# Up projection: the products with the rounded weights and those with the remainders, alternating or in two groups

## The chip, the cores and the metric

The kernel runs on one core of a Trainium2 chip. The metric is the device time of one execution in microseconds (us), the median of several runs. The profile's engines are PE (TensorE: matrix products), PEld (its weight loads, which overlap the products), DVE (VectorE), ACT (ScalarE), POOL (GpSimd) and SP (SyncE, which here only starts transfers).

## What is computed

Two layers of an encoder over 256 positions with 2048 features, all in float32. Each layer has an attention part and then a gated feed-forward part. The change lies in the first product of the latter, `h2 @ w_up`:

```python
x = x + o @ w_out[l]
h2 = rms_norm(x, ln2_g[l])
u = depthwise_conv(h2 @ w_up[l], conv_w[l], conv_b[l])
gate, up = u[..., :D_FF], u[..., D_FF:]
x = x + (jax.nn.silu(gate) * up) @ w_down[l]
```

`w_up` has 2048 rows and 2 x 5632 columns in each layer.

## The kernel before

**Two parts for each number.** A float32 operand is split into a rounded part ("hi", in a format that PE multiplies fast) and the remainder ("lo", the same format). ACT writes the rounded part (line 112 for weights, 115 for activations) and DVE the remainder (113, 116). A product is the sum of hi x hi, lo x hi and hi x lo.

**The order of the weights.** All weights pass through one list of quanta of 1 MB, in the order in which they are used. SP loads a quantum into one of three `raw` buffers; each is split in two half blocks of 1024 columns (three for the kind "seven"), into `whi` and `wlo`, of which there are five buffers each. The loop at line 853 goes through the half blocks: it issues the split of the one four steps ahead, then the products of its own, then side work that is due (transposes, scores, sums of squares). The instructions are put in their final order on each engine by the framework's scheduler, which can move products of one half block past others. A buffer is free for the next split when the last product that reads it has run.

**The up projection** (`q_up`, line 527). A block `f` has 128 columns of the gate and 128 of the up part: two quanta, four half blocks. Its result is a PSUM tile `ps` of the tag `mm` (two buffers): for each of the two column groups `j` one bank of 512 columns, the first 256 for the products of two rounded parts, the second 256 for the two mixed products. In a half block, for each `j` and each of four slices `k` of 128 features, `two` (line 411) issues two products with the weights as the stationary operand and the activations `xs[k]` as the moving one:

- the rounded weights against both parts of `xs[k]`, 512 columns, into the whole bank;
- the remainders against the rounded part of `xs[k]`, 256 columns, added to the bank's second half.

Each product has its own weight load. There are 88 blocks in the two layers, so 352 half blocks, and in each eight products of 512 and eight of 256 columns.

**What follows a block** (`glu`, line 541): ACT copies the banks' first halves (545), DVE adds the second halves (546) and multiplies by the row factors r2 (547), POOL fills the edges, ACT and DVE do the convolution and the gate (555 to 561), and the result is split into `mid` buffers. ACT's first pass waits for the last product of the block.

**Around it.** The attention part runs its projections as products of 512 columns (`three`), and its scores (line 326, `thrice`) and values as products of 256 columns in the same fast format, in between. In the feed-forward part eight (at the end twelve) up blocks make a chunk; then comes the down projection of the chunk, with products of 512 columns only, where `mid` is stationary. The first up block of a layer starts while the last quarter of `x` is still being normalised: `turn_x` transposes it (149), `prep_x` splits it into `xs12` to `xs15`, and `stat_x` spreads r2 over the partitions by a product with ones (`pv<-tq,ones`).

Of the kernel before, what the change touches and what calls it, by code (L numbers as in the profile page):

```python
# [23 lines left out]
KD = D // P  # L24
# [35 lines left out]
def encoder_kernel(  # L60
# [36 lines left out]
    def mm(ps, lhsT, rhs, start, stop):  # L97
        nc.tensor.matmul(ps, lhsT, rhs, start=start, stop=stop, skip_group_check=True)  # L98
# [27 lines left out]
    xs = {}  # L126
# [281 lines left out]
    def at(q, f, *args, half=1):  # L408
        side.setdefault((q, half), []).append((f, args))

    def two(ps, w_h, w_l, mv, first, last):

        mm(ps, w_h, mv, first, False)
        mm(ps[:, 1], w_l, mv[:, 0], False, last)

    def three(ps, terms, hv, lv, first, last, apart=False):

# [109 lines left out]
    def q_up(l, f, u):  # L527
        def body(q, half, hi, lo):
            if u == 0 and half == 0:
                cur["up"] = psum.tile([P, 2, 2, T], F32, name="mm", bufs=2)  # L530
            ps = cur["up"]
            hv, lv = (w.rearrange("p (k j n) -> p k j n", k=4, j=2) for w in (hi, lo))
            for j in range(2):
                for kk in range(4):
                    k = 8 * u + 4 * half + kk
                    two(ps[:, j], hv[:, kk, j], lv[:, kk, j], xs[k], k == 0, k == KD - 1)
            if u == 1 and half == 1:
                glu(l, f, ps)
        return body

    def glu(l, f, ps):
        ux = halo[f % 2]
        r = T // GRID_W
        t = work.tile([P, 2, T], F32, name="prob", bufs=2)
        nc.scalar.activation(t, ps[:, :, 0], AF.Copy)  # L545
        nc.vector.tensor_add(t, t, ps[:, :, 1])  # L546
        nc.vector.tensor_mul(ux[:, :, r:r + T], t, st["r2"][:, None, :].to_broadcast([P, 2, T]))  # L547

        nc.gpsimd.tensor_copy(ux[:, :, 1:r], ux[:, :, T:T + r - 1])  # L549
        nc.gpsimd.tensor_copy(ux[:, :, T + r:T + 2 * r - 1], ux[:, :, r + 1:2 * r])  # L550
        y = work.tile([P, 2, T], F32, name="pT", bufs=4)
        for j in range(2):
            c = j * NF + f
            w0, w1, w2, b = (par["conv"][:, l, i, c:c + 1] for i in range(4))
            nc.scalar.activation(y[:, j, :], ux[:, j, r:r + T], AF.Identity, scale=w1, bias=b)  # L555
            for w, o in ((w0, 0), (w2, 2 * r)):
                nc.vector.scalar_tensor_tensor(y[:, j, :], ux[:, j, o:o + T], w, y[:, j, :],  # L557
                                               op0=ALU.mult, op1=ALU.add)
        nc.scalar.activation(t[:, 0, :], y[:, 0, :], AF.Silu)  # L559
        m = work.tile([P, T], F32, name="bias", bufs=2)  # L560
        nc.vector.tensor_mul(m, t[:, 0, :], y[:, 1, :])
        gs[f] = middle(l, f)
        split(gs[f][:, 0], gs[f][:, 1], m)
        ms[f] = m
        if f % 2 and f < NF - CHUNKS[-1] + PART:
            sums_mid(l, f // 2, ms.pop(f - 1), ms.pop(f))
# [265 lines left out]
    ps = psum.tile([P, T], F32, name="pv", bufs=1)  # L832
# [128 lines left out]
```

## Time and profile before

| | |
|---|---|
| median of 3 runs | 2092.12 us (2092.11 to 2092.13) |
| profiled execution | 2092.0 us, span 2090.2 us from the first to the last instruction |
| granted TensorE clock | 1.0 |
| up products with `whi` / `wlo` | 2816 / 2816 |
| up stretches, for example | 471.57 to 560.32 us, eight blocks |

Rows of groups give line, engine, operation, tiles written and read, shapes, count, busy time, mean ns of one and idle time of the engine before them. Rows of the timeline give start, duration, engine, line, operation and tiles, and how many equal instructions in a row are merged into one; the duration then reaches from the first start to the last end. Products are pipelined, so a product's duration is longer than the time until the next one starts. Rows of waits give who waited for whom, the total, how often and the longest.

### The profile page before, as it was taken

What the parts mean: (1) busy time and instruction counts of PE and PEld (TensorE: products, weight loads), DVE (VectorE), ACT (ScalarE), POOL (GpSimd) and SP (SyncE); (2) the same over time, 40 slices, a digit from 0 to 9 for tenths busy, and PEclk for the clock granted to TensorE, in tenths of its full rate; (3) what the DMA queues carried; (4) which work ended last, traced back from release to release, by engine and by line L of the source; (5) the groups of instructions that cost most, each with busy time, mean ns of one, the idle gap of its engine ahead of it and who ended that gap; (6) DMA issues with size and microseconds to landing.
All of it is one profiled execution on the core that took longest, in us unless ns stands there. A gap on an engine that the chain in (4) does not pass through costs nothing.

```text
span 2090.2 us, 29185 instructions
## 1 busy us (share of the span) xinstructions
PE 2083.5 (100%) x10816; PEld 1789.2 (86%) x10816; DVE 1720.5 (82%) x2604; ACT 1222.3 (58%) x1817; POOL 170.3 (8%) x237
## 2 busy tenths in 40 slices
PE   9999999999999999999999999999999999999999
PEld 8888888888888888888888888888888888888887
DVE  7786757898898988989757866678989989899896
ACT  7566556555555556556555665565556555555563
POOL 0011100100101001010000011001001010010100
PEclk9999999999999999999999999999999999999999
DMA  9544555556565564655655444555555655556554
GB/s 350 199 145 164 179 172 174 198 195 211 180 241 182 208 210 167 242 193 211 208 181 181 162 160 166 177 182 189 214 202 170 236 199 204 201 185 234 185 200 161
DMA packets 62144, 408.42 MB, mean 195 GB/s; under 512 B 7344, under 2 KB 9904, under 8 KB 13744
## 3 DMA queue, kind: packets, MB, share of 16 engines
q1 hardware_dynamic: 61280, 405.46, 56.2%
q8 instruction: 85, 1.39, 0.3%
q10 hardware_dynamic: 720, 1.08, 0.2%
q14 instruction: 59, 0.48, 0.1%
HBM read 404.42 MB, written 2.10 MB: 194 GB/s over the span
## 4 chain that ended last, share of the span: by engine, by line
PE 99%; DMA 0%; ACT 0%; DVE 0%; issue 0%
PE mm L98 90%; PE S L98 4%; PE pv L98 3%; PE tr L98 2%; PE tr L373 1%; PE tr L307 1%; PE S L149 1%; DMA head<-in_head 0%; ACT qtok L274 0%; ACT kT L315 0%; ACT xs L115 0%; DVE x L688 0%; ACT whi L112 0%
## 5 line engine op out<-in xcount | busy, mean ns | idle before, releaser
L112 ACT ACTIVATE whi<-raw 128x1024 fp32r<-128x1024 f32 (+1 forms) x797 | 830.9, 1057 | 689.9 <-PE mm L98 411.9
L113 DVE TENSOR_TENSOR wlo<-raw,whi 128x1024 fp32r<-128x1024 f32 (+1 forms) x797 | 963.9, 1220 | 270.3 <-ACT whi L112 231.8
L98 PE MATMUL mm<-xs,whi 128*128 128x512 f32 x2816 | 977.0, 390 | 0.0
L98 PE MATMUL mm<-xs,wlo 128*128 128x256 f32 x2816 | 794.1, 282 | 0.0
L98 PEld LDWEIGHTS mm<-xs,whi 128*128 128x128 f32 x2816 | 528.3, 188 | 110.5
L98 PEld LDWEIGHTS mm<-xs,wlo 128*128 128x128 f32 x2816 | 532.2, 189 | 1.1
L98 PE MATMUL mm<-whi,mid 128*128 128x512 f32 x1412 | 368.2, 391 | 0.0
L98 PEld LDWEIGHTS mm<-whi,mid 128*128 128x128 f32 x1412 | 263.0, 188 | 53.9
L98 PE MATMUL mm<-whi,xs 128*128 128x512 f32 x1152 | 294.2, 393 | 1.4 <-ACT qtok L274 1.3
L98 PEld LDWEIGHTS mm<-whi,xs 128*128 128x128 f32 x1152 | 213.1, 188 | 44.7 <-ACT qtok L274 1.8
L98 PE MATMUL mm<-wlo,mid 128*128 128x512 f32 x706 | 202.4, 392 | 0.0
L98 PE MATMUL mm<-wlo,xs 128*128 128x512 f32 x576 | 159.5, 393 | 0.0
L98 PEld LDWEIGHTS mm<-wlo,mid 128*128 128x128 f32 x706 | 132.1, 188 | 27.0
L557 DVE SCALAR_TENSOR_TENSOR pT<-halo,conv,pT 128x256 f32<-128x256 f32 x352 | 148.1, 478 | 0.9
L549 POOL COPY halo<-halo 128x6 f32<-128x6 f32 x88 | 39.6, 450 | 1232.6 <-DVE halo L547 1232.6
L98 PEld LDWEIGHTS mm<-wlo,xs 128*128 128x128 f32 x576 | 107.3, 188 | 21.6
L555 ACT ACTIVATE pT<-halo,conv 128x256 f32<-128x256 f32 x176 | 95.1, 587 | 5.8 <-DVE halo L547 5.7
L550 POOL COPY halo<-halo 128x6 f32<-128x6 f32 x88 | 77.1, 876 | 0.2 <-POOL halo L549 0.2
L547 DVE TENSOR_TENSOR halo<-prob,acc_b 128x512 f32<-128x512 f32 x88 | 60.6, 689 | 1.9
L546 DVE TENSOR_TENSOR prob<-prob,mm 128x512 f32<-128x512 f32 x88 | 59.8, 679 | 0.0
L545 ACT ACTIVATE prob<-mm 128x512 f32<-128x512 f32 x88 | 51.3, 583 | 7.1 <-PE mm L98 7.1
L559 ACT ACTIVATE prob<-pT 128x256 f32<-128x256 f32 x88 | 35.5, 404 | 30.0 <-DVE pT L557 30.0
(180 smaller groups left out, 1475.4 us busy)
## 6 DMA issues: line engine op xcount, KB each, us to landing
raw<-in_w_up SPq DMA_DIRECT2D x176, 1024.0 KB, 4.9
raw<-in_w_in SPq DMA_DIRECT2D x71, 1024.0 KB, 4.9
raw<-in_w_down SPq DMA_DIRECT2D x48, 1024.0 KB, 4.8
raw<-in_w_seven SPq DMA_DIRECT2D x40, 1024.0 KB, 4.9
raw<-in_w_out SPq DMA_DIRECT2D x32, 1024.0 KB, 4.9
raw<-in_w_plain SPq DMA_DIRECT2D x10, 1024.0 KB, 4.8
bias<-in_bias SPq DMA_DIRECT2D x16, 160.0 KB, 3.1
x<-in_x SPq DMA_DIRECT2D x4, 512.0 KB, 10.7
```

Source lines behind the costliest of these rows:

```text
L98: nc.tensor.matmul(ps, lhsT, rhs, start=start, stop=stop, skip_group_check=True)
L112: high = nc.scalar.activation(hi, src, AF.Copy)
L113: nc.vector.tensor_sub(lo, src, hi.bitcast(F32))
L149: nc.tensor.transpose(ps[:, j, tt * P:(tt + 1) * P], x[:, tt, (k + j) * P:(k + j + 1) * P], ident)
L545: nc.scalar.activation(t, ps[:, :, 0], AF.Copy)
L546: nc.vector.tensor_add(t, t, ps[:, :, 1])
L547: nc.vector.tensor_mul(ux[:, :, r:r + T], t, st["r2"][:, None, :].to_broadcast([P, 2, T]))
L549: nc.gpsimd.tensor_copy(ux[:, :, 1:r], ux[:, :, T:T + r - 1])
L550: nc.gpsimd.tensor_copy(ux[:, :, T + r:T + 2 * r - 1], ux[:, :, r + 1:2 * r])
L555: nc.scalar.activation(y[:, j, :], ux[:, j, r:r + T], AF.Identity, scale=w1, bias=b)
L557: nc.vector.scalar_tensor_tensor(y[:, j, :], ux[:, j, o:o + T], w, y[:, j, :], op0=ALU.mult, op1=ALU.add)
L559: nc.scalar.activation(t[:, 0, :], y[:, 0, :], AF.Silu)
```

## The change

In each half block of the up projection the eight products with the rounded weights are issued first, in the order of `j` and `k`, and then the eight with the remainders in the same order. Operands, banks, numbers of products and flags are the same.

```diff
-    def two(ps, w_h, w_l, mv, first, last):
-
-        mm(ps, w_h, mv, first, False)
-        mm(ps[:, 1], w_l, mv[:, 0], False, last)
+    def two(terms):
+
+        for ps, w_h, w_l, mv, first, last in terms:
+            mm(ps, w_h, mv, first, False)
+        for ps, w_h, w_l, mv, first, last in terms:
+            mm(ps[:, 1], w_l, mv[:, 0], False, last)
...
-            for j in range(2):
-                for kk in range(4):
-                    k = 8 * u + 4 * half + kk
-                    two(ps[:, j], hv[:, kk, j], lv[:, kk, j], xs[k], k == 0, k == KD - 1)
+            two([(ps[:, j], hv[:, kk, j], lv[:, kk, j], xs[k], k == 0, k == KD - 1)
+                 for j in range(2) for kk, k in enumerate(range(8 * u + 4 * half, 8 * u + 4 * half + 4))])
```

PE's order in the first half block of a layer's third up block, before:

```order
L98 MATMUL mm_3322<-xs0_2795,whi_3203 128x512
L98 MATMUL mm_3322<-xs0_2795,wlo_3204 128x256
L98 MATMUL mm_3322<-xs1_2798,whi_3203 128x512
L98 MATMUL mm_3322<-xs1_2798,wlo_3204 128x256
L98 MATMUL mm_3322<-xs2_2806,whi_3203 128x512
L98 MATMUL mm_3322<-xs2_2806,wlo_3204 128x256
L98 MATMUL mm_3322<-xs3_2809,whi_3203 128x512
L98 MATMUL mm_3322<-xs3_2809,wlo_3204 128x256
```

The same half block with the change; the rows shown are its second four products with `whi` and its first four with `wlo`:

```order
L98 MATMUL mm_3322<-xs0_2795,whi_3203 128x512
L98 MATMUL mm_3322<-xs1_2798,whi_3203 128x512
L98 MATMUL mm_3322<-xs2_2806,whi_3203 128x512
L98 MATMUL mm_3322<-xs3_2809,whi_3203 128x512
L98 MATMUL mm_3322<-xs0_2795,wlo_3204 128x256
L98 MATMUL mm_3322<-xs1_2798,wlo_3204 128x256
L98 MATMUL mm_3322<-xs2_2806,wlo_3204 128x256
L98 MATMUL mm_3322<-xs3_2809,wlo_3204 128x256
```

Runs of eight equal widths take the place of the alternation, in all half blocks but the first few of each layer, where other work is mixed in.

ACT's order at the start of the first layer's up stage, where the last slices of `x` are rounded (`xs12` to `xs15`) between the splits of coming weights, before:

```order
L112 ACTIVATE whi_3107<-raw_2947 128x1024
L115 ACTIVATE xs12_3090<-S_3085,head_72 128x256
L115 ACTIVATE xs14_3101<-S_3096,head_72 128x256
L112 ACTIVATE whi_3142<-raw_3010 128x1024
L115 ACTIVATE xs13_3093<-S_3085,head_72 128x256
L115 ACTIVATE xs15_3104<-S_3096,head_72 128x256
L112 ACTIVATE whi_3162<-raw_3010 128x1024
```

With the change:

```order
L112 ACTIVATE whi_3107<-raw_2947 128x1024
L112 ACTIVATE whi_3142<-raw_3010 128x1024
L115 ACTIVATE xs12_3090<-S_3085,head_72 128x256
L115 ACTIVATE xs14_3101<-S_3096,head_72 128x256
L115 ACTIVATE xs13_3093<-S_3085,head_72 128x256
L112 ACTIVATE whi_3162<-raw_3010 128x1024
L115 ACTIVATE xs15_3104<-S_3096,head_72 128x256
```

The split `whi_3142` moved ahead of the slices and `whi_3162` ahead of `xs15`.

ACT's order at the end of a chunk, where the last up block's first pass (`prob<-mm`) stands among splits of the down projection's weights and of sums (`mid<-tq`), before:

```order
L112 ACTIVATE mid_5154<-bias_5152 128x256
L112 ACTIVATE whi_5231<-raw_5078 128x1024
L545 ACTIVATE prob_5254<-mm_5172 128x512
L112 ACTIVATE mid_5162<-tq_5157 128x256
L112 ACTIVATE whi_5273<-raw_5078 128x1024
```

With the change:

```order
L112 ACTIVATE mid_5154<-bias_5152 128x256
L112 ACTIVATE whi_5231<-raw_5078 128x1024
L112 ACTIVATE mid_5162<-tq_5157 128x256
L545 ACTIVATE prob_5254<-mm_5172 128x512
L112 ACTIVATE whi_5273<-raw_5078 128x1024
```

The sum's split and the block's first pass changed places. The orders of SP and POOL are the same in both kernels.

## The prediction

> **What bounds the kernel now.** I read the page's first and fourth parts first, then the list of waits for PE and its weight loads, then single stretches of the timeline.
>
> ```profile
> PE 2083.5 (100%) x10816; PEld 1789.2 (86%) x10816; DVE 1720.5 (82%) x2604; ACT 1222.3 (58%) x1817; POOL 170.3 (8%) x237
> PE 99%; DMA 0%; ACT 0%; DVE 0%; issue 0%
> L98 PE MATMUL mm<-xs,whi 128*128 128x512 f32 x2816 | 977.0, 390 | 0.0
> L98 PE MATMUL mm<-xs,wlo 128*128 128x256 f32 x2816 | 794.1, 282 | 0.0
> L98 PEld LDWEIGHTS mm<-xs,wlo 128*128 128x128 f32 x2816 | 532.2, 189 | 1.1
> ...
> PE mm L98 <- ACT qtok L274: 1.3, 2, 0.7
> PE pv L98 <- DVE halfpi L94: 1.1, 1, 1.1
> ...
> PEld mm L98 <- ACT whi L112: 1.0, 3, 0.4
> ```
>
> PE is the whole chain, and it waits for other engines for 2.4 us in 2090, its weight loads for a little more. The two groups that the change reorders, 2816 products with the rounded weights (512 columns, called h here) and 2816 with the remainders (256 columns, called l), have no idle time before them. So nothing that ACT, DVE or a DMA delivers sooner can be worth anything here, and the question is only the pace at which PE starts products. The durations 390 and 282 ns are no pace: products overlap, so I count from start to start. The first two rows below are the first h of one up stretch and the first product after it, 256 pairs later; the next two stand 24 products of 512 columns apart in a down stretch.
>
> ```profile
> 471.57 0.39 PE L98 MATMUL mm<-xs,whi 128*128 128x512 f32 x1
> ...
> 560.32 1.08 PE L98 MATMUL mm<-whi,mid 128*128 128x512 f32 x4
> ...
> 1001.41 1.98 PE L98 MATMUL mm<-whi,mid 128*128 128x512 f32 x8
> ...
> 1006.85 1.52 PE L98 MATMUL mm<-whi,mid 128*128 128x512 f32 x6
> ```
>
> A pair takes (560.32 - 471.57) / 256 = 0.3467 us. A 512 among its like takes (1006.85 - 1001.41) / 24 = 0.2267, which leaves 0.1200 for an l in the alternation. The up stretches hold 2816 x 0.3467 = 976 us of the span. They are already the plain sum of their parts, with not one stall to win back.
>
> **The change part by part.** No product, load, split or DMA is added or removed. There are 2816 / 8 = 352 half blocks. In each, h l h l ... (8 x 0.3467 = 2.773 us) becomes eight h and then eight l. Fifteen changes of width become one inside, and one at the seam. The price is what eight l in a row take, and what eight h take right behind them. The up stretches hold almost no such runs, so I take the nearest ones: in the attention parts, scores and values run as 256s of the same format, each with its own weight load, and eight 512s follow.
>
> ```profile
> 112.14 0.28 PE L98 MATMUL S<-kTb,qT 128*128 128x256 f32 x1
> ...
> 112.86 2.00 PE L98 MATMUL mm<-whi,xs 128*128 128x512 f32 x8
> 114.70 1.07 PE L98 MATMUL mm<-wlo,xs 128*128 128x512 f32 x4
> ...
> 1153.34 0.28 PE L98 MATMUL S<-kTb,qT 128*128 128x256 f32 x1
> ...
> 1154.05 2.00 PE L98 MATMUL mm<-whi,xs 128*128 128x512 f32 x8
> 1155.89 1.07 PE L98 MATMUL mm<-wlo,xs 128*128 128x512 f32 x4
> ...
> 1226.73 1.98 PE L98 MATMUL mm<-whi,xs 128*128 128x512 f32 x8
> 1228.54 0.39 PE L98 MATMUL mm<-wlo,xs 128*128 128x512 f32 x1
> ```
>
> The last two rows are the control: eight 512s behind 512s take 1228.54 - 1226.73 = 1.81 us. Behind six 256s they take 114.70 - 112.86 = 1.84, and in the second layer 1155.89 - 1154.05 = 1.84. The six 256s themselves take 0.72 and 0.71, 0.120 each and a little less. Six l and eight h at the old paces are 0.720 + 1.813 = 2.533; these stretches take 2.56 and 2.55, so **+0.027 and +0.017 us**. The reader is to see that a run of narrow products costs nothing itself, and that the wide ones behind it are slow for a while. Two more such places give the ends.
>
> ```profile
> 101.92 0.28 PE L98 MATMUL S<-mid,qT 128*128 128x256 f32 x1
> ...
> 102.98 1.78 PE L98 MATMUL mm<-whi,xs 128*128 128x512 f32 x7
> 104.60 0.39 PE L98 MATMUL mm<-wlo,xs 128*128 128x512 f32 x1
> ...
> 127.90 0.87 PE L98 MATMUL pv<-pT,v_b 128*128 128x256 f32 x6
> 128.61 0.39 PE L98 MATMUL mm<-wlo,xs 128*128 128x512 f32 x1
> 128.84 2.01 PE L98 MATMUL mm<-whi,xs 128*128 128x512 f32 x8
> 130.70 1.07 PE L98 MATMUL mm<-wlo,xs 128*128 128x512 f32 x4
> ...
> 172.07 0.85 PE L98 MATMUL pv<-pT,v_b 128*128 128x256 f32 x6
> 172.76 1.99 PE L98 MATMUL mm<-whi,xs 128*128 128x512 f32 x8
> ```
>
> Nine 256s and seven 512s from 101.92: 2.68 against 9 x 0.120 + 7 x 0.2267 = 2.667, +0.013. Six and nine from 127.90: 2.80 against 2.760, **+0.040**, the upper end. The six from 172.07 take 0.69 (0.115 each), and seven starts among the eight behind them take 1.99 - 0.39 = 1.60 against 1.587: -0.030 + 0.013 = **-0.017**, the lower end. That last run stands right behind transposes, unlike the others.
>
> One disturbance of the kind stands in an up stretch itself, where the scheduler put two h in a row:
>
> ```profile
> 341.98 0.63 PE L98 MATMUL mm<-xs,whi 128*128 128x512 f32 x2
> ...
> 343.61 0.39 PE L98 MATMUL mm<-xs,whi 128*128 128x512 f32 x1
> ```
>
> Between these rows start five h and four l: 1.63 us against 5 x 0.2267 + 4 x 0.120 = 1.613, +0.017 for one broken alternation. So the same tiles react too. I take the mean of the two stretches that are nearest in form, six 256s and then exactly eight 512s: +0.022 us for a half block. The sum is 352 x 0.022 = 7.7 us, on the profiled execution's 2092.0 (span 2090.2 and 1.8 around it; the median, 2092.12, is the same): **2099.7 us**. The ends are 352 x 0.040 = +14.1 and 352 x -0.017 = -6.0.
>
> [...]
>
> What moves on other engines. The split of the weights is released earlier: the last read of a whi is now 8 x 0.120 = 0.96 us before the half block's end, and no reader needs it sooner. The first l comes seven h later than it did. Neither can add a wait in steady blocks, and PE shows none to remove. At the chunks' ends ACT rounds a sum (mid<-tq) ahead of the first pass of the last block's gate (prob<-mm), not behind it.
>
> ```profile
> 560.58 0.60 ACT L545 ACTIVATE prob<-mm 128x512 f32<-128x512 f32 x1 [0.70 <-PE mm L98]
> 561.08 0.41 ACT L112 ACTIVATE mid<-tq 128x256 fp32r<-128x256 f32 x1
> ...
> 561.89 0.68 DVE L546 TENSOR_TENSOR prob<-prob,mm 128x512 f32<-128x512 f32 x1
> ...
> 565.09 0.61 PE L98 MATMUL mm<-whi,mid 128*128 128x512 f32 x2
> ```
>
> ACT stood idle 0.70 us before prob, so mid's 0.41 fits there; and PE writes the freed bank only at 565.09, 2.5 us after DVE's read ends. I cost it at nothing. Without that cover it is at most 0.41 us at each of ten chunk ends, 4 us. At the start of each layer's up stage xs15 is now rounded behind one more whi and its subtraction.
>
> ```profile
> L112 ACT ACTIVATE whi<-raw 128x1024 fp32r<-128x1024 f32 (+1 forms) x797 | 830.9, 1057 | 689.9 <-PE mm L98 411.9
> L113 DVE TENSOR_TENSOR wlo<-raw,whi 128x1024 fp32r<-128x1024 f32 (+1 forms) x797 | 963.9, 1220 | 270.3 <-ACT whi L112 231.8
> ```
>
> That is 1.06 + 1.22 us later, but the order puts 19 h and 15 l of other work (19 x 0.2267 + 15 x 0.120 = 6.1 us) between PE's row for r2 and its first product with xs15: nothing, too, and at most 2 x 2.3 = 4.6 us if that cover failed.
>
> **The rivals.** *Order does not count* (0.33): with the runs regular and all from the same tiles, PE settles, and eight and eight take 2.773 us as before. For it: the alternation is the exact sum of its parts, and no wait is touched. Against it: every place above where 256s end has slow 512s behind it. It gives 2092.0, and holds as long as a half block gains or loses under 0.012 us (4.2 us in all, 0.2%, about what a measurement of this kernel tells from no change). That the scheduler undoes the change would give the same time, but PE's order shows the runs.
>
> *The l settle faster than 0.120* (0.08), the other side: eight in a row are long enough to reach the 0.115 of the run at 172.07, and the h behind lose only 0.013. It decides in the change's favour once eight l save more than the 512s lose, 0.03 us; at -0.017 a half block it gives 2086.0. Against it: the runs of six at 112.14 and of nine at 101.92 stay at 0.118 to 0.120.
>
> *Weight loads come into the open* (0.02): a load is 189 ns by its row, an l only 120. Were the loads of seven l in a row shown in full, it would be 352 x 7 x 0.069 = 170 us more, 2262. The runs of 256s, with a load each, exclude it nearly.
>
> **How the numbers follow.** The forecast, +0.013 to +0.040 a half block or 2096.6 to 2106.1, has 0.57. With the rivals that makes slower by over 0.2% 0.59, within it 0.33, faster 0.08. The range, 2086 to 2106, takes in both ends of the unknown price and the case of no change, and leaves out about 1 in 20. The likeliest case's own range is 2096.6 to 2106.1.
>
> **What would show it.** In the profile after, the eight h of a half block, from the first's start to the first l's, should take about 1.84 us, not 1.81, and the eight l 0.94 to 0.96; the waits of PE should stay near 2.4 us, and the stretches outside the up projection keep their lengths. If the h take 1.81 and the l 0.96, the second case holds; if the l take 0.92 or less, the third. A wait of PE for xs, mid or a bank would mean that a cover costed at nothing has failed. The forecast is wrong if the slow starts come from the change of tiles or formats around the attention's products and not from the change of width.

## The result, and the profile after

The changed kernel takes **2103.97 us**, the median of four runs (2103.80 to 2103.98); the kernel before took 2092.12 in the runs beside it (2092.11 to 2092.32). The ratio is 1.0056, with a 95% interval of 1.0040 to 1.0072: slower by 11.85 us. The forecast was 2099.7 in a range of 2086 to 2106.

The first fence has rows of the page of the changed kernel: engines, the chain that ended last, and the groups that the change reorders. The second has its list of waits for PE.

```profile
PE 2094.4 (100%) x10816; PEld 1781.5 (85%) x10816; DVE 1721.8 (82%) x2604; ACT 1224.6 (58%) x1817; POOL 109.8 (5%) x237
PE 99%; DMA 0%; ACT 0%; DVE 0%; issue 0%
L98 PE MATMUL mm<-xs,whi 128*128 128x512 f32 x2816 | 714.4, 395 | 0.0
L98 PEld LDWEIGHTS mm<-xs,whi 128*128 128x128 f32 x2816 | 504.2, 188 | 97.9
L98 PE MATMUL mm<-xs,wlo 128*128 128x256 f32 x2816 | 388.4, 280 | 0.0
```

```profile
PE mm L98 <- ACT qtok L274: 1.3, 2, 0.7
PE pv L98 <- DVE halfpi L94: 1.1, 1, 1.1
PE mm L98 <- ACT whi L112: 0.9, 1, 0.9
```

PE is still the whole chain, it waits for 3.3 us instead of 2.4, and the two groups have no idle time ahead of them. A weight load lasts 188 ns, as before, and lies beside the products. The busy times of the two groups fell by hundreds of us although the kernel is slower: overlapping products of one group are counted once, so busy time says nothing of the pace here. The timeline does. Its rows give start, duration, engine and operation, and how many equal ones are merged.

```profile
112.79 2.00 PE L98 MATMUL mm<-whi,xs 128*128 128x512 f32 x8
114.63 1.07 PE L98 MATMUL mm<-wlo,xs 128*128 128x512 f32 x4
...
472.44 2.03 PE L98 MATMUL mm<-xs,whi 128*128 128x512 f32 x8
...
480.85 2.03 PE L98 MATMUL mm<-xs,whi 128*128 128x512 f32 x8
482.72 1.10 PE L98 MATMUL mm<-xs,wlo 128*128 128x256 f32 x8
483.66 2.03 PE L98 MATMUL mm<-xs,whi 128*128 128x512 f32 x8
485.53 1.10 PE L98 MATMUL mm<-xs,wlo 128*128 128x256 f32 x8
486.46 2.03 PE L98 MATMUL mm<-xs,whi 128*128 128x512 f32 x8
...
562.25 1.09 PE L98 MATMUL mm<-whi,mid 128*128 128x512 f32 x4
```

From start to start, eight h take 1.87 us (482.72 - 480.85) and eight l 0.94 or 0.93 (483.66 - 482.72, 486.46 - 485.53): 0.2337 and 0.117 each. The forecast had reckoned with 0.2267 and 0.1200 for the kernel before. The mean of all starts in the traces, from here on "by all starts", gives 0.2284 and 0.1184 there, and 0.2333 and 0.1174 with the change. The up stretch of eight blocks is 562.25 - 472.44 = 89.81 us; it was 88.75. That is 0.033 for each of its 32 half blocks, 352 x 1.06 / 32 = 11.7 us in all, nearly the whole difference. The eight 512s of the attention part, on which the forecast leaned, take 1.84 us, as before.

So the h became slower by far more than the l became faster, and the h do not settle: all eight take about 0.2337. The question is why.

### The profile page after: what moved, and what is told of

Same layout as the page of the kernel before. It is cut to its first block, busy times and chain, and to the rows that moved or that the text cites. A ratio compares the mean times of both kernels' runs of the same rounds, so it can differ in the third digit from the quotient of the medians.

```text
span 2102.1 us, 29183 instructions
## 1 busy us (share of the span) xinstructions
PE 2094.4 (100%) x10816; PEld 1781.5 (85%) x10816; DVE 1721.8 (82%) x2604; ACT 1224.6 (58%) x1817; POOL 109.8 (5%) x237
## 4 chain that ended last, share of the span: by engine, by line
PE 99%; DMA 0%; ACT 0%; DVE 0%; issue 0%
PE mm L98 90%; PE S L98 4%; PE pv L98 3%; PE tr L98 2%; PE tr L373 1%; PE tr L307 1%; PE S L149 0%; DMA head<-in_head 0%; ACT qtok L274 0%; ACT kT L315 0%; ACT xs L115 0%; DVE x L688 0%; ACT whi L112 0%
## 5 line engine op out<-in xcount | busy, mean ns | idle before, releaser
L98 PE MATMUL mm<-xs,whi 128*128 128x512 f32 x2816 | 714.4, 395 | 0.0
L98 PEld LDWEIGHTS mm<-xs,whi 128*128 128x128 f32 x2816 | 504.2, 188 | 97.9
L98 PEld LDWEIGHTS mm<-xs,wlo 128*128 128x128 f32 x2816 | 380.3, 188 | 32.2
L98 PE MATMUL mm<-xs,wlo 128*128 128x256 f32 x2816 | 388.4, 280 | 0.0
L549 POOL COPY halo<-halo 128x6 f32<-128x6 f32 x88 | 31.5, 358 | 1305.0 <-DVE halo L547 1305.0
L747 DVE TENSOR_TENSOR raw<-raw 128x1024 f32<-128x1024 f32 x40 | 48.8, 1220 | 0.5
```

What stands on the lines that cost most here:

```text
L747: nc.vector.tensor_sub(w[:, 1:3], w[:, 1:3], w[:, 2:4])
```

## The experiments

All times are of the slowest and only core; the kernel before, on the same chips, took 2092.03 to 2092.27 in all of them.

### Shorter and longer runs

Four of each kind, and two of each kind (`terms` is the list that the changed kernel hands to `two`; three points stand for lines left out):

```diff
...
+            for i in range(0, 8, 4):
+                two(terms[i:i + 4])
```

> Groups of four in place of eight: for each j four products with whi, then four with wlo, twice the seams. Theory A (a wide product that runs within about nine starts after a narrow run goes at 0.2337 us, whatever the number of seams, and a narrow one in a run at 0.117): 4 x 0.2337 + 4 x 0.1175 twice = 2.81 us for a half block as in the changed kernel, 2102 to 2105 us. Theory B (each seam between the widths has a fixed price, 0.0335 us, the changed kernel's loss for a half block): twice the loss, 352 x 0.067 = 23.6 us, 2116 us.

```diff
...
+            for i in range(0, 8, 2):
+                two(terms[i:i + 2])
```

> Groups of two: h h l l all through. Theory A: the wide ones never settle; between 0.0067 us for each h h l l, as at 339.24 us of the kernel before, and the 0.0335 for a half block of the changed kernel: 2101 to 2104 us. Theory B (fixed price for a seam, now four in a half block): 352 x 0.134 = 47 us, 2139 us.

One run each: 2101.72 and 2108.45 us. By all starts, h take 0.2332 and l 0.1168 in groups of four, 0.2343 and 0.1178 in groups of two. A fixed price for each change of width is out: the loss would have doubled and quadrupled, to 23.6 and 47 us, and it is 9.6 and 16.3.

Sixteen of each (the remainders' products kept to the end of the quantum), and 32 of each (to the end of the block):

```diff
-    def two(terms):
+    late = []
+
+    def two(terms, end):
...
-        for ps, w_h, w_l, mv, first, last in terms:
-            mm(ps[:, 1], w_l, mv[:, 0], False, last)
+        late.extend(terms)
+        if end:
+            for ps, w_h, w_l, mv, first, last in late:
+                mm(ps[:, 1], w_l, mv[:, 0], False, last)
+            late.clear()
...
+            two(terms, half == 1)
```

> The products with wlo of two half blocks are issued together: sixteen h, then sixteen l. Theory A: the wide ones settle at 0.2267 after about nine, so they lose 9 x 0.005 to 0.007 = 0.045 to 0.06 us, and the narrow ones at 0.117 save 16 x 0.003 = 0.048: 0 to +0.015 a pair of half blocks, 2091 to 2095 us. Theory B: half the seams, half the loss: 2098 us. A third possibility, that consecutive wide products of these tiles are slow for good (0.2337): 16 x 0.007 - 0.045 = 0.067 a pair, 2104 us.

The version with 32 differs from it in one condition:

```diff
-            two(terms, half == 1)
+            two(terms, u == 1 and half == 1)
```

> The products with wlo of a whole block are issued together: 32 h, then 32 l. Theory A: the wide ones lose 0.045 to 0.06 us once, the narrow ones save 32 x 0.003 = 0.09 at 0.117, or, if they settle at 0.1133 after eight, up to 0.18: 88 blocks x -0.03 to -0.14 us = 2080 to 2089 us. Theory B: a quarter of the loss, 2095 us. Slow for good: 32 x 0.007 - 0.09 = +0.13, 2104 us. All of this if the longer life of wlo makes PE wait nowhere.

They take 2107.77 us (ratio 1.0075, 1.0058 to 1.0091) and 2132.14 (1.0190, 1.0175 to 1.0206). The timeline of the version with sixteen:

```profile
482.14 2.05 PE L98 MATMUL mm<-xs,wlo 128*128 128x256 f32 x16
484.02 3.89 PE L98 MATMUL mm<-xs,whi 128*128 128x512 f32 x16
487.75 1.45 PE L98 MATMUL mm<-xs,wlo 128*128 128x256 f32 x11
```

Sixteen h take 3.73 us, 0.2331 each, and sixteen l 1.88, 0.1175 each. A slow start that fades, which is what the forecast was made of, would show a lower mean in a longer run; it shows the same. The rest of these two versions' time lies outside the pace: by all starts, the products outside the up projection take 5.5 us more than in the changed kernel with sixteen and 27.5 us more with 32. With 32 the remainders are held longer, so their buffers come free later, and PE waits for splits, as its waits show:

```profile
PE pv L98 <- ACT whi L112: 9.8, 11, 1.0
PE S L98 <- DVE wlo L113: 6.8, 10, 0.7
```

The idea that the h are slow only behind narrow products falls here. What was left: wide products of these tiles, where they lie, are slow in a row, for good. Next I asked what about them it is.

### Neighbours, and one width alone

The alternation as before, but with each remainder product taken from another slice:

```diff
...
+            for i in range(0, 8, 4):
+                for kk in range(4):
+                    ps_j, w_h, _, mv, first, _ = terms[i + kk]
+                    mm(ps_j, w_h, mv, first, False)
+                    _, _, w_l, mv, _, _ = terms[i + (kk + 3) % 4]
+                    mm(ps_j[:, 1], w_l, mv[:, 0], False, kk == 3 and u == 1 and half == 1)
```

> In each half block and column group, products of 512 and 256 columns alternate as before the change, but each remainder product belongs to another slice k than the rounded ones beside it, so that no two neighbours read the same xs tile. Theory W (the pace of a product depends on the widths beside it): a pair takes 0.347 us as before the change, 2092. Rival O (a wide product is quick only because the product beside it reads the same xs tile; 0.2337 and 0.117 else, as in the runs of eight): 2104, and 2112 if the narrow ones stay at 0.120.

2092.06 us beside 2092.03. Its up stretch, by the first h and the first product behind it:

```profile
471.44 0.39 PE L98 MATMUL mm<-xs,whi 128*128 128x512 f32 x1
...
560.19 1.08 PE L98 MATMUL mm<-whi,mid 128*128 128x512 f32 x4
```

88.75 us, as before the change. That neighbours read the same `xs` is worth nothing.

All products wide, in the changed order:

```diff
-            mm(ps[:, 1], w_l, mv[:, 0], False, last)
+            mm(ps, w_l, mv, False, last)
```

> The changed order, but the remainders are multiplied with both parts of xs, 512 columns into the whole bank, so that all products of the up projection are 512 wide (this adds the product of two remainders to the first half). Theory W (it is the neighbourhood of narrow products that sets the pace): 16 uniform products in a half block at the 0.2267 us of the other stretches, 3.63 us, 2392 in all. Rival T (consecutive wide products of these tiles run at 0.2337 whatever is near): 3.74 us, 2432.

2441.26 us. PE now also waits for a row of sums, 9.7 us in all, as the waits and the timeline show:

```profile
PE mm L98 <- DVE tq L619: 9.7, 8, 1.5
```

```profile
381.20 2.03 PE L98 MATMUL mm<-xs,wlo 128*128 128x512 f32 x8
383.07 1.09 PE L98 MATMUL mm<-xs,whi 128*128 128x512 f32 x4
```

Without that wait it would be 2431.6, and eight wide products take 1.87 us with no narrow one near. So rival T's 2432 holds: the slow pace of the h needs no change of width.

All products narrow, in the order before:

```diff
+        mm(ps[:, 0], w_h, mv[:, 0], first, False)
+        mm(ps[:, 1], w_h, mv[:, 1], False, False)
         mm(ps[:, 1], w_l, mv[:, 0], False, last)
```

> The order before the change, but each product with the rounded weights is made as two of 256 columns, one for each part of xs, so that all products of the up projection are 256 wide, 24 in a half block. If narrow ones in a row run at the 0.117 us that they take in runs of eight: 2103. If at 0.120, as in the alternation: 2129. If the 512s' 0.2267 is two halves without a cost of their own: 0.1133, 2072.

2104.35 us, the first of the three cases. The two rows are 13 times three products apart:

```profile
479.79 0.28 PE L98 MATMUL mm<-xs,wlo 128*128 128x256 f32 x1
...
484.33 0.28 PE L98 MATMUL mm<-xs,wlo 128*128 128x256 f32 x1
```

4.54 / 39 = 0.1164 us. Here 256 columns take half of 0.2337, nearly: uniform products in the up stage of these kernels go at one rate per column, and that rate is not the one of the other stages.

### The place of the weights

In the up stage alone, the split weights do not begin at the start of their buffers but `UP_AT = 56` columns behind it (line 53, used at 756), 224 bytes. Buffers of `whi` and `wlo` stand 1088 columns apart, 4352 = 17 x 256 bytes, and the tiles `xs` and `mid` whole multiples of 2048. So the distance from the moving operand to the stationary one, within 256 bytes, is the same for every product of a stage: 0 for the wide products of the attention and down parts, 224 in the up part. The changed kernel at 0:

```diff
-UP_AT = 56
+UP_AT = 0
```

> The changed kernel with the split weights at the start of their buffers in the up stages too, not 56 columns behind it. If the place of the weights against the activations is what makes consecutive wide products slow (rival P): the wide ones go back to 0.2267 us while the narrow ones keep 0.117, 20 us less, 2084. If the place does not matter: 2104 as the changed kernel.

2099.02 us, beside 2092.03: neither case. The timeline:

```profile
480.68 2.00 PE L98 MATMUL mm<-xs,whi 128*128 128x512 f32 x8
482.52 1.11 PE L98 MATMUL mm<-xs,wlo 128*128 128x256 f32 x8
483.48 2.00 PE L98 MATMUL mm<-xs,whi 128*128 128x512 f32 x8
...
489.06 2.00 PE L98 MATMUL mm<-xs,whi 128*128 128x512 f32 x8
```

Eight h take 1.84 us and eight l 0.96; three half blocks take 489.06 - 480.68 = 8.38, 2.793 each, 0.020 over the 2.773 of before, and 352 x 0.020 = 7.0 us is the whole difference. This is the attention part's behaviour, which the forecast had taken for granted: by the trace's starts, in both, the h settle from 0.236 at most to 0.227 over five products, and the 256s take 0.120. It appears in the up stage once the weights have the attention part's place.

Then two kernels with many places, and with room made for moving the `xs` too:

```diff
-UP_AT = 56
+UP_AT = (40, 0, 2, 4, 6, 8, 10, 12, 14, 24, 32)
+XS_AT = 8
...
-        xs[k] = act.tile([P, 2, T], F32R, name=f"xs{k}")
+        o = XS_AT if which == 1 and l == 1 else 0
+        xs[k] = act.tile([P, 2 * T + 16], F32R, name=f"xs{k}")[:, o:o + 2 * T].rearrange("p (a t) -> p a t", a=2)
...
-            o = UP_AT if kind == "up" else 0
-            hl[s] = tuple(wp.tile([P, 1024 + 64], F32R, name=t, bufs=SPLIT_AHEAD + 1)[:, o:o + 1024]
+            o = UP_AT[ups.index(s) % 176 // 16] if kind == "up" else 0
+            hl[s] = tuple(wp.tile([P, 1024 + 48], F32R, name=t, bufs=SPLIT_AHEAD + 1)[:, o:o + 1024]
```

> The changed order; the offset of the split weights in their buffers changes every four up blocks, in each layer 40, 0, 2, 4, 6, 8, 10, 12, 14, 24 and 32 columns of 4 bytes (all buffers begin 32 bytes behind a multiple of 64, so 8, 24 and 40 begin on a multiple and 0 and 32 half way), and in the second layer the xs of the up projection are moved by 8 columns, onto a multiple of 64 bytes. Theory D (the place of the weights within 64 bytes sets the pace of products in runs): 8, 24 and 40 show eight h in 1.87 and eight l in 0.935 us, 0 and 32 show 1.84 and 0.955, in both layers alike, what lies between is open. Rival E (the place of weights and xs against each other): in the second layer the two kinds change sides. Rival F (the place within 256 bytes or more): 8, 24 and 40 differ from each other. In all about 2101.

The same edit on the kernel before:

> The order before the change with the same offsets of weights and xs by stretch. If the alternation does not care for the place: eight pairs take 2.77 us in every stretch, 2092. If the alternation too takes the slow pace for the wide or the narrow ones at some places: up to 8 x (0.2337 + 0.120) = 2.83 us in those stretches, and between 2092 and 2110 in all.

2120.46 and 2118.42 us, both above what was expected, and no pattern by offset: in every stretch of both, means of 0.231 to 0.234 for h and 0.117 to 0.119 for l. But the whole kernel was slower, by 19 us outside the up products (by all starts in the trace), and that is what the run taught. The room for `xs` had cost each weight buffer 16 columns. They now stood 4288 bytes apart and the `xs` 2112, and the distance within 256 bytes changed by 64 from buffer to buffer, and from `xs` to `xs`. Of the 19 us, 7 lie in the attention part's products with `xs`, and most of the rest in the down projection's. Down stretches, where `whi` is the moving operand and the `mid` buffers keep one place within 256 bytes (the line numbers are one higher in this kernel):

```profile
1345.09 2.02 PE L99 MATMUL mm<-whi,mid 128*128 128x512 f32 x8
1346.94 1.09 PE L99 MATMUL mm<-wlo,mid 128*128 128x512 f32 x4
...
1351.11 2.00 PE L99 MATMUL mm<-whi,mid 128*128 128x512 f32 x8
1352.94 1.07 PE L99 MATMUL mm<-wlo,mid 128*128 128x512 f32 x4
1353.85 2.03 PE L99 MATMUL mm<-whi,mid 128*128 128x512 f32 x8
1355.72 1.09 PE L99 MATMUL mm<-wlo,mid 128*128 128x512 f32 x4
```

The three groups of eight have the distances 128, 0 and 64 (from the buffers' places) and take 1.85, 1.83 and 1.87 us; in the kernel before such a group takes 1.81. Single groups scatter: over all of four products or more with `whi` in the down stretches, a product takes 0.2293 on average at 0, 0.2326 at 64 and 128 and 0.2300 at 192, and 0.2274 in the kernel before. I had changed the layout and the offset at once, so neither theory D nor E nor F could be read from it. The clean version keeps every buffer in its place:

```diff
-UP_AT = 56
+UP_AT = (56, 0, 4, 8, 12, 16, 20, 24, 28, 32, 36, 40, 44, 48, 52, 60, 64, 2, 6, 10, 30, 58)
...
-            two([(ps[:, j], hv[:, kk, j], lv[:, kk, j], xs[k], k == 0, k == KD - 1)
-                 for j in range(2) for kk, k in enumerate(range(8 * u + 4 * half, 8 * u + 4 * half + 4))])
...
+            if l == 0:
+                two(terms)
+            else:
+                for t in terms:
+                    two([t])
...
-            o = UP_AT if kind == "up" else 0
+            o = UP_AT[ups.index(s) % 176 // 8] if kind == "up" else 0
```

> All buffers where the kernels before and after have them; the offset of the split weights changes every two up blocks, in each layer 56, 0, 4, 8 ... 52, 60, 64, 2, 6, 10, 30, 58 columns of 4 bytes. In the first layer the changed order, in the second the order before. Theory G (what counts is the distance from the moving to the stationary operand within 256 bytes, the same for all products of a stretch here, but not in the run before, e9_places, where the moved buffers made it change from product to product): at 0 and 64, a distance of 0, eight h settle to 1.82 to 1.84 us and eight l take 0.955; at 56 1.87 and 0.935; at 16, 32 and 48, as in the down stretches of the run before at these distances, 512s of 0.233, 0.2315 and 0.2295, so 1.86, 1.85 and 1.84. Rival H (the distance is nothing; the run before was slow for another reason in its layout): all stretches of the first layer 1.87 and 0.935. For the alternation: 0.347 a pair at 56, at the others nothing is known, 0.347 to 0.354. In all 2090 to 2112.

2101.42 us. In its timeline, the first layer's stretches at offsets 0, 36 and 48 columns, and two rows of the second layer's alternation at offset 0, 61 pairs apart:

```profile
367.06 2.00 PE L98 MATMUL mm<-xs,whi 128*128 128x512 f32 x8
368.90 1.12 PE L98 MATMUL mm<-xs,wlo 128*128 128x256 f32 x8
369.85 2.00 PE L98 MATMUL mm<-xs,whi 128*128 128x512 f32 x8
...
639.65 2.03 PE L98 MATMUL mm<-xs,whi 128*128 128x512 f32 x8
641.52 1.12 PE L98 MATMUL mm<-xs,wlo 128*128 128x256 f32 x8
642.47 2.03 PE L98 MATMUL mm<-xs,whi 128*128 128x512 f32 x8
...
761.83 2.00 PE L98 MATMUL mm<-xs,whi 128*128 128x512 f32 x8
763.66 1.07 PE L98 MATMUL mm<-xs,wlo 128*128 128x256 f32 x8
764.57 1.99 PE L98 MATMUL mm<-xs,whi 128*128 128x512 f32 x8
766.40 1.10 PE L98 MATMUL mm<-xs,wlo 128*128 128x256 f32 x8
767.34 0.40 PE L98 MATMUL mm<-xs,whi 128*128 128x512 f32 x1
...
1399.42 0.40 PE L98 MATMUL mm<-xs,whi 128*128 128x512 f32 x1
...
1420.97 0.40 PE L98 MATMUL mm<-xs,whi 128*128 128x512 f32 x1
```

A half block in the changed order takes 2.79 us at 0, 2.82 at 36, and 2.74 and 2.77 in turn at 48. In the alternation eight pairs at 0 take 8 x (1420.97 - 1399.42) / 61 = 2.826. By all starts in a stretch, for six of the offsets, and for 56 from the kernels after and before:

| offset, columns | eight h and eight l | eight pairs, alternating |
|---|---|---|
| 0 | 2.790 | 2.826 |
| 16 | 2.779 | 2.826 |
| 24 | 2.816 | 2.775 |
| 36 | 2.827 | 2.794 |
| 48 | 2.763 | 2.826 |
| 56 (kernels after and before) | 2.807 | 2.773 |
| 64 | 2.789 | 2.826 |

Rival H falls. Theory G holds in that the place sets the pace, but its numbers, carried over from the down stretches, were wrong in part: at 16 and 48 the l, which have no counterpart there, take 0.115 and 0.116. And the two orders do not like the same places. At 56, 24 and 36 the alternation is quicker, at 0, 16 and 48 the runs of eight. Offsets of 0 and 64, 256 bytes apart, agree in both. Over all 22, the alternation is never under the 2.773 that it has at 56, and the runs of eight are clearly under it only at 48.

### A version faster than both

```diff
-UP_AT = 56
+UP_AT = 48
```

> The changed kernel with the split weights 48 columns into their buffers in all up stages, the offset at which eight and eight took least in the run before (2.763 us on the average of its two blocks, against 2.807 at 56 and 2.773 in the kernel before). Theory G (the distance sets the pace, and the same distance gives the same pace everywhere): 352 x (2.763 - 2.773) = 3.5 us less than the kernel before, 2088.6, faster than both. Rival J (a stretch of two blocks does not tell the pace of whole stages, because the pace depends on what ran before too): 2.78 to 2.81, 2094 to 2105.

**2086.15 us** (2085.98 to 2086.95), beside 2092.08; the ratio is 0.9972, 95% interval 0.9962 to 0.9983. Its timeline in an up stretch:

```profile
482.01 2.00 PE L98 MATMUL mm<-xs,whi 128*128 128x512 f32 x8
483.85 1.07 PE L98 MATMUL mm<-xs,wlo 128*128 128x256 f32 x8
484.75 1.99 PE L98 MATMUL mm<-xs,whi 128*128 128x512 f32 x8
486.58 1.11 PE L98 MATMUL mm<-xs,wlo 128*128 128x256 f32 x8
487.52 2.00 PE L98 MATMUL mm<-xs,whi 128*128 128x512 f32 x8
```

Two half blocks (487.52 - 482.01) take 5.51 us, 2.755 each, 0.018 under the 2.773 of before; 352 x 0.018 = 6.3 us, of which 5.9 were measured. Theory G's direction and place hold, rival J falls, and the size was 2.4 us more than forecast.

## Why the prediction was right, and where it was not

**Held.** PE is the whole chain, the question is only the pace, and the change costs by the slower h: sign and place of the loss are those of the forecast. That the sign held is in part luck, though: the same change of order costs at 56, 24 and 36 columns and gains at 0, 16 and 48, and the forecast gave no thought to the offset. Weight loads stay hidden. ACT's moves, costed at nothing, added at most the 0.9 us wait for `whi`. No other stretch was touched: of the 11.85 us, 11.7 are 352 times what a half block lost.

**The mis-sized term** is the +0.022 us for a half block; it measured +0.033. The step that failed is the choice of its source: "I take the mean of the two stretches that are nearest in form, six 256s and then exactly eight 512s". They are nearest in form, but their operands stand at a distance of 0 within 256 bytes, and those of the up stage at 224. (The 256s of the values, from which both ends of the range came, stand at 64.) With the weights at 0, eight and eight in the up stage do take 0.020 more than the 2.773 of the kernel before (2099.02 us); but that kernel has its weights at 56, and at 0 its alternation takes 2.826. At 224 bytes eight and eight do something else: the h do not start slowly and settle, they stay at about 0.2337.

The two prices of the alternation, from which the loss was counted, were not measured there either. 0.2267 is the pace of the down stretches, and 0.1200 what it leaves of 0.3467. By all starts the alternation's h take 0.2284 and its l 0.1184. With the change they take 0.2333 and 0.1174, and 8 x (0.0049 - 0.0010) = 0.031 of the 0.033: the loss is the h's, and the l give back a fifth of it.

**The mechanism was wrong in part, too.** "The wide ones behind it are slow for a while" is no effect of the width in the up stage: with no narrow product near they were as slow, and they stay so. The prediction named this among what would make it wrong, with tiles and formats as the causes; the cause was neither, but the place of the weights in their buffers. *The l settle faster* had the l right, 0.117 at once, but they had taken 0.1184 already, so little was saved, and it was wrong in what it assumed of the h. *Order does not count* is refuted at this offset, and holds as little at the others, where it counts in either direction. The alternation's "plain sum of their parts" was also read too far: 0.3467 is the price at this offset and a few others, pairs take up to 0.353 elsewhere, and eight and eight at 48 take less than eight pairs at any offset tried.

The Trainium skill, "TensorE: Matmul & The Clock Gate", section Back-to-back issue gap, gives N / 2.4 + 2.5 ns as the gap of an isolated product of N columns at full clock, some 216 ns at 512, and says that in a stream of weight loads and products both set the spacing, with about 131 ns at 512 columns measured. Here a product of 512 columns in such a stream took 227 ns at the least on average, and eight and eight of the same widths, with the same loads, took 2.74 to 2.83 us by place and order; the measurement decides. "SBUF — State Buffer", section Operand start alignment, says that an operand must start at a multiple of its element size, and that this is a matter of legality, not of speed. All offsets here are such multiples, and between them lie up to 0.06 us in 2.8.

**Open.** Why the place counts is open. That it is the distance between the two operands, as theory G has it, is not shown either, but the place of one of them alone does not set the pace: the first `whi` buffer begins at the same byte in the kernel before and in the first run with moved buffers (2120.46 us), and as the moving operand of the down stretches it takes 0.2276 us for a product in the one and 0.2328 in the other, where the `mid` buffers stand elsewhere; and with `mid` at one place within 256 bytes, the five `whi` buffers of that run take 0.2293 to 0.2328. The pace also hangs on what ran before, as the settling h at 0 show. Nor was it tried whether whi and wlo would do better at two different places, for example 48 and 16, or what the kernel before takes as a whole at other offsets; two blocks of each gave nothing quicker than 56. That the change would gain some (2.826 - 2.790) x 352 = 13 us if both kernels had the weights at 0 is worked out from two blocks of each, and not run.

## What to carry to other kernels

In this kernel, where PE is the whole chain and hardly waits, the order of its products is not neutral, but what it is worth hangs on where the operands lie; a price taken from another stage is not safe unless the operands have the same places there, and one that is left over from a subtraction should be measured by itself. So an offset that was chosen for one order has to be looked for again with the next: one kernel that gives each stretch its own offset shows them all in one trace. And whoever varies a place keeps all other buffers where they were: 16 columns less in each of ten weight buffers, and 16 more in each `xs`, cost 19 us in stages that the edit was not about.

## What had not been expected of the hardware

By the stretches of these traces, the pace of a 128x512 product in this fast format went from 0.2267 to about 0.237 us, and that of a 128x256 from 0.113 to 0.121, with the granted clock at 1.0 and no wait of PE in those stretches, by a few dozen bytes in the place of the weights and by the order. At 48, eight l took 0.91 us (764.57 - 763.66) behind every other group of h, and 0.94 to 0.95 behind the rest, in stable turn.
